# A hybrid layer on one core: differential attention weights carried to float32r tiles and transposed there, a mask on GpSimd, later transposes of the memory

## The chip, the cores and the metric

The kernel runs on one core of a Trainium2 chip. The metric is device time in microseconds (us) for one execution; the time given is the median of several runs. Five engines work in parallel, each in the order of its own instruction list: TensorE (PE), VectorE (DVE), ScalarE (ACT), GpSimd (POOL) and SyncE (SP), whose list issues nearly all transfers here. An engine that meets an instruction whose input or buffer isn't ready stands still, and everything behind it in that list stands with it.

## The reference

One layer, 1024 tokens of width 1024, float32. Three branches read the same normalised input and are merged by gates; the sum goes through an output matrix and a norm, and is added to the input. Cut to what the change touches:

```python
h = rms_norm(x, pre_w)                       # 1024 x 1024; then ten blocks of h @ w_in
# gated DeltaNet, 8 heads of 128, chunks: decay factors of a chunk, lower triangle only
gamma = jnp.exp(jnp.where(incl, G[..., :, None] - G[..., None, :], -jnp.inf))
# differential attention, 8 heads with two maps of width 64, 8 query blocks of 128
sc = jnp.einsum("bqhmd,bkhmd->bhmqk", q[:, start:end], k[:, :end]) * scale
p = jax.nn.softmax(sc + bias[None, :, None], axis=-1)
pd = (p[:, :, 0] - lam * p[:, :, 1])
outs.append(jnp.einsum("bhqk,bkhe->bqhe", pd, v[:, :end]))
# cross attention into a fixed memory of 256 rows
m = rms_norm(mem, mem_norm_w)
mk, mv = jnp.split(m @ w_mem_kv, 2, axis=-1)
# merge
y = gates[:, :, 0] * y_gdn + gates[:, :, 1] * y_diff + gates[:, :, 2] * y_mem
return x + rms_norm(y @ w_out, post_w)
```

## The kernel before, in words

The big products run in float32r. A weight block is loaded as float32, cast to a high part on ACT (line 167, `wh`) and its remainder is formed on DVE (line 169, `wl`); three matmuls for each piece (lines 219, 220, 224) then replace one of full precision.

The main program issues these products in order. Everything else is written as generators, threads that yield; a thread goes on by a step after a fixed number of the main program's matmuls, `pause(n)` waits for n steps, and a scheduler then settles the order of each engine's list when the program is built. So the order on each engine is fixed before the run, and a thread's instruction that comes too early for its input stops the engine.

The span has these stages. Up to about 545 us: the DeltaNet projections (`zmul` is the last kind of them), with threads for keys and queries (function `decay` loads decay rows, adds the mask `mneg`, and takes eight exponentials, line 468, in one go), for a triangular inverse, and for the scan over chunks (its end normalises two heads at a time on POOL, lines 691 and 692). From 545 to 680 us: `zmul(6)` and `zmul(7)`, beside them `mem_norm` (the memory's rows are normalised at line 760 and transposed at line 767) and `combine_tokens` (adds on POOL, lines 818 to 821, and on DVE), then the memory's values and keys (lines 795 to 797). From 680 to 1560 us: the other projections by a Strassen scheme (line 878, 3024 matmuls of 512 columns), and one thread that runs the 8 attention heads one after the other, then the memory's. From 1560 us: three branch products, the output product and the last norm.

In a head of the attention, query block i has w = 128 (i+1) keys. `scores(i)` makes both maps' scores in PSUM (lines 1142 and 1143) and adds the bias on DVE (line 1146); `exps(i)` takes both exponentials on ACT (line 1158); `combine(i)` forms p0 - lam p1 on DVE (line 1167); `turn(i)` transposes that on PE in blocks of 128 columns as plain float32 (line 1176), up to four blocks to a PSUM bank, and copies them back; `values(i)` multiplies them by v (line 1191). `turn` and `values` run one block behind `scores`. The head's v itself is transposed by `turned` (line 720), which uses float32r operands. A matmul operand of type float32r has to be written as such by its producer; a transfer can do that, since it copies bits.

Of the kernel before, what the change touches and what calls it, by code (L numbers as in the profile page):

```python
# [9 lines left out]
F32 = mybir.dt.float32  # L10
# [6 lines left out]
P = 128  # L17
# [28 lines left out]
def bm(ap, m):  # L46

    return ap.unsqueeze(1).to_broadcast([ap.shape[0], m, ap.shape[1]])
# [3 lines left out]
def hybrid_layer_kernel(  # L52
# [148 lines left out]
    def pause(n):  # L201
        for _ in range(n):
            yield
# [72 lines left out]
    with gx:  # L276
# [8 lines left out]
        tri = gp.tile([P, P], F32, name="tri")  # L285
        G.memset(tri, 1.0)
        G.affine_select(tri, tri, pattern=[[1, P]], compare_op=ALU.is_ge, fill=0.0, base=0, channel_multiplier=-1)
        mneg = gp.tile([P, P], F32, name="mneg")
        G.memset(mneg, 0.0)
        G.affine_select(mneg, mneg, pattern=[[1, P]], compare_op=ALU.is_ge, fill=NEG, base=0, channel_multiplier=-1)  # L290
        ones = gp.tile([P, P], F32, name="ones")
        G.memset(ones, 1.0)

# [167 lines left out]
        def decay(h, gm):  # L461

            nc.sync.dma_start(gm, gscr[0, 8 * h:8 * h + 8, :].rearrange("c i -> (c i)").partition_broadcast(P))
            yield from pause(2)
            V.tensor_tensor(gm, gm, bm(mneg, 8), op=ALU.add)
            yield from pause(1)
            for c in range(8):
                A.activation(gm[:, c], gm[:, c], AF.Exp, bias=negG[:, h, c:c + 1])
# [249 lines left out]
    def turned(out_, in_):  # L718

        T.transpose(out_.bitcast(F32R), in_, identr)  # L720

    def xtile(shape=(P, S), dt=F32):
        return xp.tile(list(shape), dt, name=nm("x"), tag="x", bufs=9)
# [20 lines left out]
    def mem_norm():  # L744

        mts = []
        for t in range(2):
            mt = rtile((P, D))
            nc.sync.dma_start(mt, mem[t * P:(t + 1) * P, :])
            mts.append(mt)  # L750
        for _ in range(2):
            mh.append(xtile((P, 4, MEM), F32R))
            ml.append(xtile((P, 4, MEM), F32R))
        sq = rtile()
        for mt in mts:
            ss = small([P, 1], "ss", 4)
            A.activation(sq, mt, AF.Square, accum_out=ss)
            rs = small([P, 1], "rs", 4)
            rpow(rs, ss, 1.0 / D, EPS, mhalf)
            V.tensor_scalar(mt, mt, rs, None, op0=MUL)  # L760
            yield
        yield from pause(3)
        for k2 in range(4):
            pt = sd()
            for kk in range(2):
                for t in range(2):
                    T.transpose(pt[:, 2 * kk + t], mts[t][:, (2 * k2 + kk) * P:(2 * k2 + kk + 1) * P], ident)
            for kk in range(2):
                k = 2 * k2 + kk
                src = pt[:, 2 * kk:2 * kk + 2].rearrange("p a b -> p (a b)")  # L770
                A.activation(mh[k // 4][:, k % 4], src, AF.Copy, scale=memw[:, k:k + 1])
                V.scalar_tensor_tensor(ml[k // 4][:, k % 4], src, memw[:, k:k + 1],
                                       mh[k // 4][:, k % 4].bitcast(F32), op0=MUL, op1=SUB)
            yield
        ready.add("mem")
# [317 lines left out]
    def diff_head(h):  # L1093
# [57 lines left out]
        def exps(i):  # L1151
            w = (i + 1) * P
            ng = small([P, 2], "ng", 4)
            V.tensor_scalar(ng, mxs.pop(i)[:, (w - 1) // 512], -scl, None, op0=MUL)  # L1154
            yield
            l1 = l1s[i] = small([P, 1], "l1", 4)
            for m, l in enumerate((l0[:, i:i + 1], l1)):
                A.activation(s[i][m][:, :w], s[i][m][:, :w], AF.Exp, bias=ng[:, m:m + 1], scale=scl, accum_out=l)  # L1158
                yield from pause(2)

        def combine(i):
            w = (i + 1) * P
            s0, s1 = s[i]
            c1 = small([P, 1], "c1", 4)
            V.reciprocal(c1, l1s.pop(i))
            V.scalar_tensor_tensor(c1, c1, l0[:, i:i + 1], nlam, op0=MUL, op1=MUL)
            V.scalar_tensor_tensor(s0[:, :w], s1[:, :w], c1, s0[:, :w], op0=MUL, op1=ADD)

        def turn(i):

            pT = s[i][1].rearrange("p (a b) -> p a b", b=P)
            for b in range(0, i + 1, 4):
                n = min(4, i + 1 - b)
                pp = sd()
                for c4 in range(n):
                    T.transpose(pp[:, c4], s[i][0][:, (b + c4) * P:(b + c4 + 1) * P], ident)  # L1176
                yield
                if b == 0:
                    A.copy(pT[:, b:b + n], pp[:, :n])
                else:  # L1180
                    V.tensor_copy(pT[:, b:b + n], pp[:, :n])
                yield

        def values(i):
            nonlocal o
            if i == 0:
                o = xtile((P, 8, P))
            pT = s.pop(i)[1].rearrange("p (a b) -> p a b", b=P)
            po = sd()
            for c in range(i + 1):  # L1190
                T.matmul(po[:, 0], lhsT=pT[:, c], rhs=vt[:, c], start=(c == 0), stop=(c == i))  # L1191
            yield from pause(2)
            A.copy(o[:, i], po[:, 0])
            A.activation(po[:, 0], po[:, 0], AF.Square, accum_out=sso[:, i:i + 1])
            yield

        for i in range(NT + 1):
            if i < NT:
                yield from scores(i)
            if i:  # L1200
                yield from turn(i - 1)
            if i < NT:
                yield from exps(i)
            if i:
                yield from values(i - 1)
            if i < NT:
                yield
                combine(i)
                yield from pause(3 if i < 2 else 1)
        spawn(diff_norm(h, o, l0, sso))  # L1210

    def diff_norm(h, o, l0, sso):
# [216 lines left out]
    for t in range(NT):  # L1429

        ts_ = slice(t * P, (t + 1) * P)
        po = pos[t] if t < 2 else columns()
        xr, res = xtile(), xtile()
        nc.sync.dma_start(xr, x[ts_, :])
        ss = small([P, 2], "oss", 4)
        for f, sl in enumerate(half):
            products(po, t, range(4 if t < 2 else 0, KT), f)
            A.activation(res[:, sl], po[f], AF.Square, scale=1.0 / 32, accum_out=ss[:, f:f + 1])
        rs = small([P, 1], "rs", 4)
        V.tensor_scalar(rs, ss[:, 0:1], ss[:, 1:2], EPS, op0=ADD, op1=ADD)  # L1440
        G.tensor_tensor(rs, rs, mhalf[:, 0:1], op=ALU.pow)
        for f, sl in enumerate(half):
            V.scalar_tensor_tensor(res[:, sl], po[f], rs, pw[:, sl], op0=MUL, op1=MUL)
            (V if f else G).tensor_tensor(res[:, sl], res[:, sl], xr[:, sl], op=ADD)
            nc.sync.dma_start(out[ts_, sl], res[:, sl])


# [22 lines left out]
```

## Time and profile before

| what | value |
|---|---|
| time, median of 3 runs | 1926.06 us (1922.33 to 1928.35) |
| profiled execution, its own time | 1924.15 us |
| span of that execution | 1922.4 us |
| PE busy | 1868.7 us, 97% of the span |
| DVE, ACT, POOL busy | 63%, 47%, 9% |
| mean granted TensorE clock | 0.99 |
| DMA, mean | 147 GB/s, 47.4% of 16 engines' time |

Busy time of PE is close to the span, so the time that PE stands still is the small difference, and it lies in few places. The other engines' busy shares say only that none of them is full on the mean; whether one of them is late at a given place is seen in the timeline there. The profiled execution's span and its own time differ by 1.75 us, which lie around the span.

### The profile page before, as it was taken

Reading aid. Unit: us, or ns where it says so; the run is one execution under the profiler, and the core shown is the slowest. Engines: PE = TensorE matmul, PEld = TensorE weight load, DVE = VectorE, ACT = ScalarE, POOL = GpSimd, SP = SyncE. Lnnn points to the kernel's source line nnn. Section 1 sums busy time; section 2 is a strip of 40 time slices with the busy share of each in tenths; the row PEclk is TensorE's granted clock in tenths of the full one; section 3 lists DMA queues with packets and bytes.
Section 4 is the critical chain, followed back from the end, with each engine's and each line's share of the span. In section 5 each row is a group of like instructions: output and inputs, shape, how many; then the busy total and the mean of one; then the engine's idle time right before and its main releaser. Section 6 shows DMA issues by size and latency. Waiting matters only on the chain.

```text
span 1922.4 us, 28495 instructions
## 1 busy us (share of the span) xinstructions
PE 1868.7 (97%) x10231; PEld 1561.9 (81%) x10231; DVE 1218.5 (63%) x2499; ACT 894.5 (47%) x1997; POOL 164.0 (9%) x131
## 2 busy tenths in 40 slices
PE   7999999999978999999999999999999999999998
PEld 5787888788866888888888888888888878888886
DVE  5688667855366676777777777766666662435432
ACT  5552664545444465555555565555444551212211
POOL 1130131302140100000000000000000000000011
PEclk9999999999989999999999999999999999999999
DMA  4232231322136675656657355443665586755422
GB/s 129 87 97 68 69 96 42 98 63 75 51 120 200 190 210 171 173 162 184 185 143 212 114 176 170 148 154 104 214 207 188 170 270 206 231 195 171 156 91 88
DMA packets 294018, 282.45 MB, mean 147 GB/s; under 512 B 41474, under 2 KB 226164, under 8 KB 293876
## 3 DMA queue, kind: packets, MB, share of 16 engines
q1 hardware_dynamic: 293876, 280.63, 47.4%
q8 instruction: 80, 1.31, 0.3%
q14 instruction: 62, 0.51, 0.1%
HBM read 189.27 MB, written 91.29 MB: 146 GB/s over the span
## 4 chain that ended last, share of the span: by engine, by line
PE 57%; issue 30%; DVE 8%; ACT 2%; DMA 2%; POOL 1%; SPq 0%; POOLq 0%; DVEq 0%; ACTq 0%
PE bank L878 27%; PE acc L224 4%; PE acc L220 4%; PE acc L219 4%; PE sd L1191 3%; PE sd L1143 2%; PE sd L1142 2%; PE sd L1176 2%; DVE o L437 1%; DVE wl L169 1%; PE sd L474 1%; DMA wr<-in_w_mem_kv_dram 1%; PE sd L661 1%; PE sd L673 1%; PE sd L668 1%
## 5 line engine op out<-in xcount | busy, mean ns | idle before, releaser
L878 PE MATMUL bank<-h,hi 128*128 128x512 f32 x864 | 283.7, 398 | 0.0
L167 ACT CAST wh<-wr 128x512 fp32r<-128x512 f32 x144 | 89.3, 620 | 281.6 <-PE acc L220 251.6
L219 PE MATMUL acc<-h,wh 128*128 128x512 f32 x468 | 194.1, 415 | 2.2 <-DVE rp L157 1.8
L220 PE MATMUL acc<-h,wh 128*128 128x512 f32 x468 | 186.7, 399 | 0.0
L878 PE MATMUL bank<-q,hi 128*128 128x512 f32 x576 | 186.4, 397 | 0.0
L878 PE MATMUL bank<-o,hi 128*128 128x512 f32 x576 | 185.2, 396 | 0.8 <-DVE u L965 0.4
L878 PEld LDWEIGHTS bank<-h,hi 128*128 128x128 f32 x864 | 159.5, 188 | 28.2
L878 PE MATMUL bank<-h,lo 128*128 128x512 f32 x432 | 171.4, 397 | 0.0
L224 PE MATMUL acc<-h,wl 128*128 128x512 f32 x468 | 159.4, 399 | 9.2 <-DVE wl L169 9.2
L169 DVE TENSOR_TENSOR wl<-wr,wh 128x512 fp32r<-128x512 f32 x144 | 102.7, 714 | 101.3 <-ACT wh L167 97.8
L864 ACT CAST hi<-wr 128x512 fp32r<-128x512 f32 x144 | 89.0, 618 | 133.2 <-PE bank L878 112.9
L868 DVE TENSOR_TENSOR lo<-wr,hi 128x512 fp32r<-128x512 f32 x144 | 98.9, 687 | 52.8 <-PE bank L878 39.8
L878 PEld LDWEIGHTS bank<-o,hi 128*128 128x128 f32 x576 | 106.4, 188 | 22.1 <-ACT u L883 1.2
L878 PEld LDWEIGHTS bank<-q,hi 128*128 128x128 f32 x576 | 107.0, 188 | 19.9
L878 PE MATMUL bank<-q,lo 128*128 128x512 f32 x288 | 114.5, 398 | 0.0
L878 PE MATMUL bank<-o,lo 128*128 128x512 f32 x288 | 114.2, 396 | 0.0
L224 PEld LDWEIGHTS acc<-h,wl 128*128 128x128 f32 x468 | 88.4, 191 | 29.1 <-DVE wl L169 11.3
L1158 ACT ACTIVATE x<-x,ng 128x256 f32<-128x256 f32 (+7 forms) x128 | 98.8, 774 | 24.7 <-DVE ng L1154 24.7
L864 ACT CAST hi<-raw 128x512 fp32r<-128x512 f32 x108 | 66.9, 619 | 84.9 <-PE bank L878 79.6
L219 PEld LDWEIGHTS acc<-h,wh 128*128 128x128 f32 x468 | 89.3, 191 | 17.4 <-issue 3.0
L220 PEld LDWEIGHTS acc<-h,wh 128*128 128x128 f32 x468 | 89.3, 191 | 14.5
L878 PEld LDWEIGHTS bank<-h,lo 128*128 128x128 f32 x432 | 81.4, 188 | 14.2
(361 smaller groups left out, 4125.3 us busy)
## 6 DMA issues: line engine op xcount, KB each, us to landing
raw<-in_w_in_dram SPq DMA_DIRECT2D x144, 256.0 KB, 3.8
wr<-in_w_in_dram SPq DMA_DIRECT2D x64, 256.0 KB, 2.8
qd<-u SPq DMA_DIRECT2D x128, 128.0 KB, 2.4
wl<-qd SPq DMA_DIRECT2D x64, 256.0 KB, 3.5
gts<-u SPq DMA_DIRECT2D x48, 256.0 KB, 3.2
u<-oscr SPq DMA_DIRECT2D x48, 256.0 KB, 4.6
raw<-gts SPq DMA_DIRECT2D x24, 512.0 KB, 4.4
o<-gscr SPq DMA_DIRECT2D x16, 512.0 KB, 4.9
```

What stands on the lines that cost most here:

```text
L167: A.copy(hi, raw)
L169: V.tensor_tensor(lo, raw, hi.bitcast(F32), op=ALU.subtract)
L219: T.matmul(ps[:, sl], lhsT=hi[:, kk], rhs=hh(k, f), start=(k == 0), stop=False)
L220: T.matmul(ps[:, sl], lhsT=hi[:, kk], rhs=hl(k, f), start=False, stop=False)
L224: T.matmul(ps[:, sl], lhsT=lo[:, kk], rhs=hh(k, f), start=False, stop=(k == 7))
L864: A.copy(self.hi[p], self.src[p])
L868: V.tensor_tensor(self.lo[p], self.src[p], self.hi[p].bitcast(F32), op=SUB)
L878: T.matmul(ps, lhsT=t[l][:, kk], rhs=comb[p][kk][r], start=(first and kk + n == 0), stop=(kk == 3 and n == 2), skip_group_check=True)
L1142: T.matmul(ps[m], lhsT=q4[:, m], rhs=ks[m][:, u:e], start=True, stop=False)
L1143: T.matmul(ps[m], lhsT=q4[:, 2 + m], rhs=ks[m][:, u:e], start=False, stop=True)
L1158: A.activation(s[i][m][:, :w], s[i][m][:, :w], AF.Exp, bias=ng[:, m:m + 1], scale=scl, accum_out=l)
L1191: T.matmul(po[:, 0], lhsT=pT[:, c], rhs=vt[:, c], start=(c == 0), stop=(c == i))
```

## The change

Five edits.

1. The mask of `decay`: the add of a tile of large negative numbers on DVE is replaced by a select on GpSimd (POOL) on the decay tile itself, 128x1024, 16 times; the mask tile `mneg` is no longer built.
2. `mem_norm` waits 9 steps in place of 3 before the transposes of the memory.
3. `combine(i)` is followed by a transfer `move(i)` on SP, which copies the weights' tile, 128 partitions by w float32, into a float32r tile of the same core's memory; 64 such transfers in all, 64 KB to 512 KB. `turn(i)` transposes the copy with `turned`, and the transposed blocks go to the tile that the weights were formed in. For w over 512 the second map's tile is given up before the copy's is taken.
4. In the loop over query blocks `exps(i)` stands right after `scores(i)`, `combine(i)` after `turn(i-1)`; the pause at a block's end is 2 steps for the first four blocks (before: 3 for two blocks, 1 for the others), and a step lies before each transfer.
5. In the last norm the product with the norm's weight is taken on DVE before the row's factor is known, the squares go back into PSUM, and one operation on DVE does the factor and the residual; before, a DVE operation and an add on POOL or DVE did.

```diff
-            V.tensor_tensor(gm, gm, bm(mneg, 8), op=ALU.add)
+            G.affine_select(gm, gm, pattern=[[0, 8], [1, P]], compare_op=ALU.is_ge, fill=NEG, base=0,
+                            channel_multiplier=-1)
...
-        yield from pause(3)
+        yield from pause(9)
         for k2 in range(4):
             pt = sd()
...
             V.scalar_tensor_tensor(s0[:, :w], s1[:, :w], c1, s0[:, :w], op0=MUL, op1=ADD)
+            del s0, s1
+            if w <= 512:
+                yield from move(i, s[i][0], xtile((P, 512), F32R))
+            else:
+                s[i][1] = None
+                yield from move(i, s[i][0], xtile(dt=F32R))
+
+        def move(i, src, dst):
+            w = (i + 1) * P
+            yield
+            s[i] = [src, dst]
+            nc.sync.dma_start(dst[:, :w].bitcast(F32), src[:, :w])
...
-                    T.transpose(pp[:, c4], s[i][0][:, (b + c4) * P:(b + c4 + 1) * P], ident)
+                    turned(pp[:, c4], s[i][1][:, (b + c4) * P:(b + c4 + 1) * P])
...
             if i < NT:
                 yield from scores(i)
+                yield from exps(i)
             if i:
                 yield from turn(i - 1)
             if i < NT:
-                yield from exps(i)
+                yield from combine(i)
             if i:
                 yield from values(i - 1)
-            if i < NT:
-                yield
-                combine(i)
-                yield from pause(3 if i < 2 else 1)
+            if i < 4:
+                yield from pause(2)
...
-            A.activation(res[:, sl], po[f], AF.Square, scale=1.0 / 32, accum_out=ss[:, f:f + 1])
+            V.tensor_tensor(res[:, sl], po[f], pw[:, sl], op=MUL)
+            A.activation(po[f], po[f], AF.Square, scale=1.0 / 32, accum_out=ss[:, f:f + 1])
...
-            V.scalar_tensor_tensor(res[:, sl], po[f], rs, pw[:, sl], op0=MUL, op1=MUL)
-            (V if f else G).tensor_tensor(res[:, sl], res[:, sl], xr[:, sl], op=ADD)
+            V.scalar_tensor_tensor(res[:, sl], res[:, sl], rs, xr[:, sl], op0=MUL, op1=ADD)
```

Lines of the changed kernel are named by its own numbers: the mask is line 462, the exponentials behind it 465, the scan's end 689 and 690, the memory's transposes 765, `turned` 718, the transfer 1177, the score products 1140 and 1141, the values 1201.

Three places of the engines' lists. First POOL, in the DeltaNet stage, where the scan's end of two heads (the two powers `sso` and the two scalings of `v`) stands. Before:

```order
L691 TENSOR_TENSOR sso_1862<-sso_1862,mhalf 128x8
L692 TENSOR_TENSOR v_1105<-v_1105,sso_1862 128x1024
L691 TENSOR_TENSOR sso_1863<-sso_1863,mhalf 128x8
L692 TENSOR_TENSOR v_1331<-v_1331,sso_1863 128x1024
L158 TENSOR_TENSOR nk<-rp_2607,phalf 128x8
L504 TENSOR_TENSOR o_2512<-o_2512,fj 128x1024
```

and now, where the three rows L462 are masks of decay tiles `o`:

```order
L689 TENSOR_TENSOR sso_1871<-sso_1871,mhalf 128x8
L690 TENSOR_TENSOR v_1110<-v_1110,sso_1871 128x1024
L689 TENSOR_TENSOR sso_1872<-sso_1872,mhalf 128x8
L690 TENSOR_TENSOR v_1338<-v_1338,sso_1872 128x1024
L462 AFFINE_SELECT o_2525<-o_2525 128x1024
L462 AFFINE_SELECT o_2648<-o_2648 128x1024
L462 AFFINE_SELECT o_2801<-o_2801 128x1024
```

The first mask of these, that of the tenth decay tile, now waits behind both powers and both scalings; before it was on DVE and waited for none of them.

Second PE, near the end of `zmul(6)`, where the memory's transposes (`raw` is a normalised memory tile) stood before; `acc_5237` is the accumulator of `zmul(6)`, `wl_5295` its second weight tile:

```order
L224 MATMUL acc_5237<-h_135,wl_5295 128x512 x2
L767 MATMUL sd_5317<-ident,raw_5250 128x128
L767 MATMUL sd_5332<-ident,raw_5250 128x128
L219 MATMUL acc_5237<-h_137,wh_5293 128x512
L220 MATMUL acc_5237<-h_138,wh_5293 128x512
L219 MATMUL acc_5237<-h_137,wh_5293 128x512
L220 MATMUL acc_5237<-h_138,wh_5293 128x512
L767 MATMUL sd_5317<-ident,raw_5252 128x128
L767 MATMUL sd_5317<-ident,raw_5250 128x128
```

Now they stand inside `zmul(7)` (`acc_5363`), behind the last product with its first weight tile `wl_5368`:

```order
L219 MATMUL acc_5363<-u_129,wh_5366 128x512
L220 MATMUL acc_5363<-u_130,wh_5366 128x512
L224 MATMUL acc_5363<-h_128,wl_5368 128x512
L224 MATMUL acc_5363<-u_129,wl_5368 128x512
L765 MATMUL sd_5402<-ident,raw_5277 128x128
L765 MATMUL sd_5402<-ident,raw_5279 128x128
L765 MATMUL sd_5402<-ident,raw_5277 128x128
L765 MATMUL sd_5402<-ident,raw_5279 128x128
L219 MATMUL acc_5363<-h_131,wh_5416 128x512
L220 MATMUL acc_5363<-h_132,wh_5416 128x512
L219 MATMUL acc_5363<-h_131,wh_5416 128x512
```

The transposes moved past the 6 matmuls that were left of `zmul(6)` and 24 of `zmul(7)`, and all four of a group now stand together.

Third SP, between the transfers of the first head's tiles 6 and 7 (both L1177); L1104 loads queries, L979 and L990 store the pieces of a later head's keys and queries, which have just left PSUM:

```order
L1177 DMA x_7158<-x_7068 128x896
L1104 DMA wl_7436<-qd_5221 128x512
L979 DMA kd_866_5208<-u_7204 64x512
L979 DMA kd_867_5209<-u_7204 64x512
L979 DMA kd_866_5208<-u_7205 64x512
L979 DMA kd_867_5209<-u_7205 64x512
L990 DMA qd_5222<-u_7239 64x4x128 x4
L990 DMA qd_5222<-u_7240 64x4x128 x4
L1177 DMA x_7276<-x_7178 128x1024
```

The second L1177 row stands behind one load and twelve stores; its transposes on PE wait for it. Before there was no transfer between a tile's weights and its transposes.

## Rows read from the trace of the kernel before

**Rows 1.** Windows: busy us of PE, PEld, DVE, ACT, POOL; granted clock, DMA share, GB/s.

```profile
545.00:680.00 135.00, 117.76 (x586) 95.81 (x586) 95.08 (x143) 64.41 (x117) 28.39 (x19) 0.95 0.60 181
...
680.00:1560.00 880.00, 876.39 (x4524) 735.77 (x4523) 619.02 (x1383) 477.38 (x1121) 13.14 (x8) 1.00 0.56 171
```

**Rows 2.** Timeline of PE, four stops: start, duration; idle before and releaser in brackets.

```profile
275.61 0.47 PE L219 MATMUL acc<-h,wh 128*128 128x512 f32 x1 [1.76 <-DVE rp L157]
...
365.41 1.22 PE L224 MATMUL acc<-h,wl 128*128 128x512 f32 x2 [4.46 <-DVE wl L169]
...
557.57 0.66 PE L767 MATMUL sd<-ident,raw 128*128 128x128 f32 x2 [8.97 <-issue]
...
579.42 0.80 PE L796 MATMUL acc<-wl,x 128*128 128x512 f32 x1 [2.89 <-DVE wl L169]
```

**Rows 3.** Groups of line 1176 and of line 720: duration ns min/median/max, first and last start.

```profile
L1176 PE MATMUL sd<-ident,x x288: 270/272/323, 681.3 to 1358.6; 128*128 128x128 f32 x144
...
L720 PE MATMUL sd<-identr,wh x64: 221/235/257, 677.1 to 1280.1; 128*128 128x128 f32 x64
```

**Rows 4.** Timeline of PE, four transposes of each kind and their neighbours.

```profile
677.05 0.45 PE L720 MATMUL sd<-identr,wh 128*128 128x128 f32 x4
677.34 0.69 PE L878 MATMUL bank<-o,hi 128*128 128x512 f32 x2
...
1000.95 0.40 PE L878 MATMUL bank<-q,lo 128*128 128x512 f32 x1
1001.18 0.60 PE L1176 MATMUL sd<-ident,x 128*128 128x128 f32 x4
1001.54 0.71 PE L878 MATMUL bank<-h,hi 128*128 128x512 f32 x2
```

**Rows 5.** Head 3, tile 7: last score product, weights formed (L1167), transposes (L1176).

```profile
1000.04 0.39 PE L1143 MATMUL sd<-x,wl 128*128 128x512 f32 x1
...
L1167 DVE SCALAR_TENSOR_TENSOR x<-x,c,x x1: 1285/1285/1285, 1007.7 to 1007.7; 128x1024 f32<-128x1024 f32 x1
...
L1176 PE MATMUL sd<-ident,x x8: 271/272/273, 1010.0 to 1011.7; 128*128 128x128 f32 x8
```

**Rows 6.** DMA issues of the page: operation, count, KB each, us to landing.

```profile
qd<-u SPq DMA_DIRECT2D x128, 128.0 KB, 2.4
...
raw<-gts SPq DMA_DIRECT2D x24, 512.0 KB, 4.4
```

**Rows 7.** Timeline of SP's queue: eight small stores in a row.

```profile
950.07 5.45 SPq L992 DMA_DIRECT2D qd<-u  x8
```

**Rows 8.** Groups of the mask add (line 465) and of a mask on GpSimd (L1075).

```profile
L465 DVE TENSOR_TENSOR o<-o,mneg x16: 1204/1224/2918, 62.6 to 442.3; 128x1024 f32<-128x1024 f32 x16
...
L1075 POOL TENSOR_SCALAR_AFFINE_SELECT x<-x x1: 1149/1149/1149, 634.8 to 634.8; 128x1024 f32<-128x1024 f32 x1
```

**Rows 9.** Timeline of POOL and ACT around two masks.

```profile
268.72 1.90 POOL L692 TENSOR_TENSOR v<-v,sso 128x1024 f32<-128x1024 f32 x1
...
350.94 4.08 POOL L692 TENSOR_TENSOR v<-v,sso 128x1024 f32<-128x1024 f32 x2
...
267.18 2.45 ACT L468 ACTIVATE o<-o,negG 128x128 f32<-128x128 f32 x8 [3.12 <-DVE o L465]
```

**Rows 10.** Timeline of DVE: one form of add at two speeds.

```profile
547.96 1.77 DVE L742 TENSOR_TENSOR o<-hi,o 128x512 fp32r<-128x512 f32 x1
549.65 0.68 DVE L742 TENSOR_TENSOR o<-lo,o 128x512 fp32r<-128x512 f32 x1
```

**Rows 11.** Timeline of DVE: a memory row normalised, a weight of the memory projection.

```profile
558.48 0.75 DVE L760 TENSOR_SCALAR raw<-raw,rs 128x1024 f32<-128x1024 f32 x1 [0.45 <-POOL rs L158]
...
578.69 0.68 DVE L169 TENSOR_TENSOR wl<-wr,wh 128x512 fp32r<-128x512 f32 x1
```

**Rows 12.** Timeline of DVE at the end of the span.

```profile
1916.61 1.41 DVE L1443 SCALAR_TENSOR_TENSOR x<-sd,rs,x 128x512 f32<-128x512 f32 x2 [0.66 <-POOL rs L1441]
...
1918.05 1.20 DVE L1444 TENSOR_TENSOR x<-x,x 128x512 f32<-128x512 f32 x1
```

More of the change, by code (lines that the diff above doesn't have):

```diff
@@ L287, in hybrid_layer_kernel @@
         G.affine_select(tri, tri, pattern=[[1, P]], compare_op=ALU.is_ge, fill=0.0, base=0, channel_multiplier=-1)
-        mneg = gp.tile([P, P], F32, name="mneg")
-        G.memset(mneg, 0.0)
-        G.affine_select(mneg, mneg, pattern=[[1, P]], compare_op=ALU.is_ge, fill=NEG, base=0, channel_multiplier=-1)
         ones = gp.tile([P, P], F32, name="ones")
@@ L1167, in combine @@
             V.scalar_tensor_tensor(s0[:, :w], s1[:, :w], c1, s0[:, :w], op0=MUL, op1=ADD)
+            del s0, s1
[9 more added lines that the diff above has]
+            nc.sync.dma_start(dst[:, :w].bitcast(F32), src[:, :w])
         def turn(i):
-            pT = s[i][1].rearrange("p (a b) -> p a b", b=P)
+            pT = s[i][0].rearrange("p (a b) -> p a b", b=P)
             for b in range(0, i + 1, 4):
@@ L1187, in values @@
                 o = xtile((P, 8, P))
-            pT = s.pop(i)[1].rearrange("p (a b) -> p a b", b=P)
+            pT = s.pop(i)[0].rearrange("p (a b) -> p a b", b=P)
             po = sd()
```

## Prediction

> **What bounds the kernel now.** The windows come first. From 680 to 1560 us, the Strassen stage with the attention beside it, PE is busy for 876.4 of 880 us at a granted clock of 1.00 [rows 1]: whatever is taken from PE's own work there shortens the span, and whatever makes PE wait there lengthens it. Between 545 and 680 us PE is busy for only 117.8 of 135 us, at a clock of 0.95 [rows 1]. Next I read the timeline of PE for its stops. Four of them matter: 8.97 us before the memory's transposes at 557.57, 2.89 us for a weight remainder from DVE at 579.42, 4.46 us for another one at 365.41, and 1.76 us at 275.61 [rows 2]. So the change has three fields: the cost of a transpose, what waits in the attention, and the stops outside it.
>
> **Transposes.** 288 float32 transposes (line 1176) become float32r ones, as the 64 of line 720 are now. Alone, a row lasts 272 against 235 ns in the median [rows 3], but neighbours overlap, so the distance to the next matmul counts. Four float32 ones hold it up from 1001.18 to 1001.54, 0.36 us; four float32r ones from 677.05 to 677.34, 0.29 us [rows 4]. That is 0.07 us for four, 18 ns each, and 288 x 18 ns = **-5.2 us**. The durations' difference of 37 ns would give -10.7; nothing at all is the other end. I take the distance, since both groups stand between the same kind of products.
>
> **The transfers.** Each tile's weights now go through SP and a transfer before PE may transpose them. I read head 3, tile 7. Its last score product starts at 1000.04, the weights are formed at 1007.7 + 1.285 = 1008.99, and the first transpose starts at 1010.0 [rows 5]. So the chain takes 8.95 us, PE has 9.96 us of other work ahead of the transpose, and the margin is 1.0 us. The changed list gives PE nearly the same work between the two: 32 products at 0.23 us (the step from 1000.95 to 1001.18 [rows 4]), seven transposes, seven products with v, together about 9.6 us. Counted in this way, the tile 7s of heads 0 to 7 have 13.9, 11.4, 13.9, 9.6, 10.5, 11.6, 9.6 and 10.2 us.
>
> No transfer of this kind is in the trace. The nearest rows are 2.4 us from issue to landing for 128 KB and 4.4 us for 512 KB [rows 6]; a last tile is 512 KB, tiles 1 to 6 lie between. With 2.4 us the chain needs 11.35 us, and PE stops for 1.75 + 0.85 + 1.75 + 1.15 = 5.5 us in heads 3, 4, 6 and 7. With 4.4 us it needs 13.35, and the sum over heads 1 and 3 to 7 is 1.95 + 3.75 + 2.85 + 1.75 + 3.75 + 3.15 = 17.2 us. Two things speak for the lower part: the two exponentials now stand ahead of the previous tile's copy on ACT, which shortens the chain, and head 3's is among the longest chains, so others need less. Tiles 0 to 6 have more time: their weights are smaller and their margin larger, and I give them nothing. I take **+7 us**.
>
> The queue is a second price. SP spends 5.45 us on eight stores, 0.68 us each [rows 7]. Behind one load and twelve stores, as tile 7 of head 0 stands, a transfer could issue up to 13 x 0.68 = 8.8 us late if the stores are released only then; in the lists some ten of 64 transfers stand behind eight or more. Most of these stores are released before the weights are formed, and head 0 has the largest supply, 13.9 us. In the sum this is nothing; in the upper end it is 5 us. The stores queued behind a waiting transfer feed tiles a head later, so their delay costs nothing as long as it stays under a head's time.
>
> **The mask.** The add took 1.22 us of DVE, 16 times [rows 8], 20 us in all; a select of the same size on GpSimd took 1.15 [rows 8]. The price lies in the list. The tenth mask now stands behind two powers and two scalings, the last of which ends at 268.72 + 1.90 = 270.6 [rows 9]. The select then ends at about 271.8 and its eight exponentials, 2.45 us, at about 274.2, where they ended at 267.18 + 2.45 = 269.6 before [rows 9]: 4.6 us late. Behind them on ACT are an operation of the convolution and a weight cast, and PE stops there already, until 275.61 [rows 2]. That stop grows by 2.5 to 4.6 us; I take 3.5. The 13th mask waits likewise until 350.94 + 4.08 = 355.0 [rows 9] and ends at 356.2. PE reaches the stop there only at 365.41 - 4.46 = 360.95 and waits for DVE, not ACT [rows 2], so I count nothing, at most 2. The freed DVE time can shorten this stop a little, and I take -0.5. Together **+3 us**, range 0 to 7.
>
> How much is DVE relieved? A two-input add of 128x512 took 0.68 us, and 1.77 while POOL was adding too [rows 10], 1.09 us more. A select on GpSimd beside such an add may thus cost back what the removed mask gave: 16 x 1.09 = 17 of 20 us. The Trainium skill, page "SBUF — State Buffer", section "Who interferes with whom", says so as a rule: a DVE instruction with two inputs in SBUF and a GpSimd instruction that reads SBUF share a port, and the later one waits for the whole of the other. By that rule the relief is 3 us of DVE time, without it 20. The two speeds in the trace agree with it.
>
> **The memory.** PE stops at 557.57 - 8.97 = 548.60 [rows 2]. In the new list 30 matmuls of 0.23 us come ahead of the transposes, so PE reaches them at about 555.5, later where the first of `zmul(7)`'s weights is late. The second normalised tile is there at 558.48 + 0.75 = 559.2 [rows 11]. So of 9 us some 3.7 stay, and 5.3 are won here. But after that PE already waits for DVE: the memory projection's weight is ready at 578.69 + 0.68 = 579.4 [rows 11], where PE stood still for 2.89 us [rows 2]. DVE works through the same list in between, and is busy for 95 us of this stage [rows 1]; a PE that comes 5 us earlier waits 5 us longer unless DVE is earlier too. I take **-1.5 us**, range 0 to -5.3.
>
> **The end.** The last two row operations and the add ran from 1916.61 to 1918.05 + 1.20 = 1919.25 [rows 12], 2.64 us; two operations of the first kind take 1.41 [rows 12]. That wins 1.2, and the squares now wait for the product ahead of them, about 0.7: **-0.5 us**, range 0 to -1.2. The mask tile that is no longer built costs nothing: its build lies beside the first loads.
>
> **Sum.** -5.2 + 7 + 3 - 1.5 - 0.5 = +2.8 us. On the profiled execution's own 1924.15 us (a span of 1922.4 and 1.75 around it) that is 1927; on the median of the runs, 1926.06, which is 0.1% higher, 1929. I forecast **1928 us**, no change that can be told.
>
> **Rivals.**
> - Faster: the transfers land behind other work after all. If the chain becomes shorter by as much as a short landing costs, the last tiles stop for 1 us in all, the memory's gain of 5.3 is kept because DVE has room, and the mask costs nothing: -5.2 + 1 - 5.3 - 0.5 = -10, 1916 us. For it speaks that margins other than the last tile's are larger; against it the 1.0 us in head 3 and the DVE list.
> - Slower: the landing decides. At 4.4 us each last tile is late as worked out: -5.2 + 17.2 + 3 - 1.5 - 0.5 = +13, 1940 us; with 5 more for the queue 1945. It ends beyond no change from a landing of about 3 us on, if the chain before it is as long as now. For it speaks the only 512 KB row; against it the two points above.
> - The change doesn't do what it says: float32r transposes of these tiles take as long as float32 ones. Then the 5.2 us are missing: +8, 1935 us. The 64 rows of line 720 speak against it.
>
> **How the numbers follow.** About 0.3%, 5.8 us, is what a measurement of this kernel can tell from no change. Chances: the forecast 0.38, faster 0.30, slower 0.24, no cheaper transposes 0.08. The forecast's own spread of some 6 us puts 0.03 of it on the faster side and 0.05 on the slower; of the faster rival 0.03 and of the slower one 0.03 stay within; of the last case half. That gives faster 0.30, same 0.37, slower 0.33 after rounding. The range runs from 1913, a little beyond the faster rival, to 1943, between the two ends of the slower one.
>
> **What would show it.** In the changed profile: four transposes of line 718 in the attention with 0.29 us to the next matmul, or 0.36; idle time of PE ahead of line 718 at tile 7 of heads 3, 4, 6 and 7 and none in heads 0 and 2; the landing time of the 512 KB copies; the stop at about 275 us grown to about 5; exponentials of the tenth mask ending at about 274; the 8.97 us stop gone, with a stop at the memory's weights of some 8 us in its place; 1.4 us in place of 2.6 at the end. The forecast is wrong if landings are far from 3 us, if DVE lets the memory's gain through, or if a late tile holds up the exponentials of the next and so the whole thread.

## The result and the profile after

The changed kernel takes 1937.45 us (median of 4 runs, 1935.62 to 1939.80), the kernel before 1927.19 in the same comparison. The ratio is 1.0056, with a 95% interval of 1.0041 to 1.0072: **10 us slower**, and clear of noise. The time lies inside the predicted range, 9 us over the forecast. It is near the figure of the slower rival, but late transfers, that rival's mechanism, are not what made it slow. One execution of the kernel before and one of c8 below took 2331 us, at a granted clock of 0.75; they are left out of every median and interval here.

The profiled execution took 1936.44 us with a span of 1934.4, 12.0 more than before. PE's first Strassen product starts at 625.3 us, where it was 614.4 before, and the last one at 1577.7, where it was 1564.7. So 10.9 of the 12 us are lost ahead of the first Strassen product.

First the windows, of the kernel before in two stretches that were not shown,

```profile
100.00:160.00 60.00, 59.00 (x299) 49.02 (x298) 54.67 (x106) 28.34 (x51) 18.81 (x15) 1.00 0.29 79
...
260.00:300.00 40.00, 37.55 (x215) 32.02 (x214) 24.40 (x59) 25.11 (x58) 15.89 (x8) 1.00 0.31 89
```

and of the changed kernel in the same two, then in its stage of the memory and its Strassen stage (columns as in [rows 1]):

```profile
100.00:160.00 60.00, 52.30 (x251) 42.82 (x250) 45.30 (x102) 31.62 (x51) 21.05 (x18) 0.94 0.26 71
...
260.00:300.00 40.00, 34.97 (x189) 29.51 (x188) 19.43 (x48) 24.23 (x54) 16.68 (x12) 0.96 0.29 83
...
555.00:692.00 137.00, 120.32 (x589) 96.21 (x588) 94.97 (x143) 63.87 (x117) 28.16 (x19) 0.94 0.59 180
...
692.00:1572.00 880.00, 872.58 (x4521) 729.81 (x4520) 617.56 (x1382) 474.82 (x1120) 13.47 (x8) 1.00 0.61 192
```

Between 100 and 160 us PE now works for 52.3 us in place of 59.0, at a clock of 0.94 in place of 1.00; between 260 and 300 us for 35.0 in place of 37.6. The stage of the memory gave 117.8 of 135 us before [rows 1] and gives 120.3 of 137 now. The Strassen stage is busy for 872.6 of 880 us.

The stops of PE in the changed kernel, in its timeline (as [rows 2]):

```profile
116.28 0.50 PE L219 MATMUL acc<-h,wh 128*128 128x512 f32 x1 [1.24 <-ACT wh L167]
...
121.84 0.79 PE L224 MATMUL acc<-h,wl 128*128 128x512 f32 x1 [4.36 <-DVE wl L169]
...
280.51 0.50 PE L219 MATMUL acc<-h,wh 128*128 128x512 f32 x1 [1.75 <-ACT wh L167]
...
284.98 0.77 PE L219 MATMUL acc<-h,wh 128*128 128x512 f32 x1 [3.28 <-DVE rp L157]
...
587.16 0.80 PE L793 MATMUL acc<-wh,x 128*128 128x512 f32 x1 [3.50 <-ACT wh L167]
591.34 0.79 PE L794 MATMUL acc<-wl,x 128*128 128x512 f32 x1 [3.39 <-DVE wl L169]
...
1100.47 0.89 PE L718 MATMUL sd<-identr,x 128*128 128x128 f32 x8 [1.55 <-DMA x<-x]
...
1269.77 0.54 PE L718 MATMUL sd<-identr,x 128*128 128x128 f32 x4 [1.67 <-DMA x<-x]
```

Before, there was no stop at 116 to 122 us. The one at 275 us (1.76 us, and 0.69 behind it for a weight remainder) has become 1.75 + 3.28. The 8.97 us stop ahead of the memory's transposes is gone; stops of 3.50 and 3.39 us at the memory's values stand in its place. In the attention, PE waits for a transfer (`DMA x<-x`), 1.55 and 1.67 us at two of the last tiles.

**The first loss** begins on ACT, 10 us ahead of the stop. The timeline of ACT before, with two masks' exponentials (eight each) between two weight casts:

```profile
104.02 0.62 ACT L167 CAST wh<-wr 128x512 fp32r<-128x512 f32 x1 [3.80 <-PE acc L220]
...
106.92 2.46 ACT L468 ACTIVATE o<-o,negG 128x128 f32<-128x128 f32 x8
...
110.24 2.44 ACT L468 ACTIVATE o<-o,negG 128x128 f32<-128x128 f32 x8
112.58 0.61 ACT L167 CAST wh<-wr 128x512 fp32r<-128x512 f32 x1
```

and after:

```profile
105.17 0.40 ACT L466 ACTIVATE o<-o,negG 128x128 f32<-128x128 f32 x1 [2.98 <-POOL o L462]
105.59 1.28 ACT L436 ACT_TABLE_LOAD   x1
106.88 1.06 ACT L436 ACTIVATE o<-o 128x1024 f32<-128x1024 f32 x1
107.96 1.28 ACT L466 ACT_TABLE_LOAD   x1
109.26 2.16 ACT L466 ACTIVATE o<-o,negG 128x128 f32<-128x128 f32 x7
...
112.28 2.44 ACT L466 ACTIVATE o<-o,negG 128x128 f32<-128x128 f32 x8
114.62 1.10 ACT L432 ACTIVATE v<-acc,cols 128x1024 f32<-128x1024 f32 x1
115.62 1.13 ACT L167 CAST wh<-wr 128x512 fp32r<-128x512 f32 x2
```

The fourth mask's exponentials (line 466 by the trace, not 465) start earlier, since the select is done sooner, but only one of the eight stands there: then comes an activation of the convolution (line 436), with a table load ahead of it and another behind, then the other seven. The weight cast that stood first, at 104.02, now stands last, at 115.62, behind both masks and another convolution activation, and PE stops for 1.24 us for it. Its remainder, which DVE formed at 108.16 before, follows only at 121.14. The cast is done at about 116.2; DVE's list has three operations of the convolution (line 434) and small ones ahead of the remainder, and DVE works through them without a pause. The longer stop, 4.36 us until 121.84, waits for that:

```profile
119.84 1.27 DVE L434 SCALAR_TENSOR_TENSOR v<-acc,cols,v 128x1021 f32<-128x1021 f32 x1
...
121.14 0.64 DVE L169 TENSOR_TENSOR wl<-wr,wh 128x512 fp32r<-128x512 f32 x1
```

No engine is full here: DVE is busy for 45.3 of these 60 us, ACT for 31.6. With the select on GpSimd the scheduler has written the lists of ACT and DVE in another order, and the cast and the remainder that PE needs next have come behind work that PE does not need.

The stops have a second price. Behind them PE's granted clock is at its lower level, 0.50 or 1.2 GHz, until about 127.5 us. Six matmuls run in two microseconds there, ten once it is 1.00 again:

```profile
124.00:126.00 2.00, 2.00 (x6) 1.52 (x6) 0.47 (x1) 0.00 (x0) 2.00 (x4) 0.50 0.31 53
...
128.00:130.00 2.00, 2.00 (x10) 1.66 (x9) 0.49 (x1) 0.62 (x1) 0.46 (x1) 1.00 0.85 246
```

The twelve products from 122.43 to 127.50 take 5.1 us; at 0.23 us each they would take 2.8, so by this estimate the clock costs some 2 us more.

**The second loss** is the one that the prediction worked out. The timelines of POOL and of ACT at the tenth mask:

```profile
273.52 1.90 POOL L690 TENSOR_TENSOR v<-v,sso 128x1024 f32<-128x1024 f32 x1
275.38 3.19 POOL L462 TENSOR_SCALAR_AFFINE_SELECT o<-o 128x1024 f32<-128x1024 f32 x3
```

```profile
276.50 2.45 ACT L466 ACTIVATE o<-o,negG 128x128 f32<-128x128 f32 x8 [6.67 <-POOL o L462]
...
279.86 1.13 ACT L167 CAST wh<-wr 128x512 fp32r<-128x512 f32 x2
```

The select waits behind the scan's last scaling until 275.4, ACT stands still for 6.67 us for it, and the exponentials, the convolution and two casts follow. Before, the exponentials ended at 269.6 [rows 9], here at 278.95, 9.3 us later. The scan's scaling itself ends 4.8 us later than before (275.4 against 270.6), since the whole stage is late by then; the other 4.5 us are the wait behind it, for which the prediction had worked out 4.6.

**The attention.** From the list of DMA issues, the transfers of 512 KB (us to landing last), and in PE's timeline head 3's tile 7, from its last score product to the first four new transposes and the matmul behind them; then the weights formed (L1165) and all the new transposes (L718):

```profile
x<-x SPq DMA_DIRECT2D x8, 512.0 KB, 4.1
```

```profile
1003.71 0.39 PE L1141 MATMUL sd<-x,wl 128*128 128x512 f32 x1
...
1013.49 0.46 PE L718 MATMUL sd<-identr,x 128*128 128x128 f32 x4
1013.78 0.46 PE L876 MATMUL bank<-q,hi 128*128 128x512 f32 x1
```

```profile
L1165 DVE SCALAR_TENSOR_TENSOR x<-x,c,x x1: 1283/1283/1283, 1008.7 to 1008.7; 128x1024 f32<-128x1024 f32 x1
```

```profile
L718 PE MATMUL sd<-identr,x x288: 218/233/327, 695.4 to 1356.7; 128*128 128x128 f32 x144
```

The 512 KB copies land in 4.1 us, near the upper end that was assumed. But the chain ahead of them has become shorter: in head 3, tile 7, from the score product at 1003.71 to the weights at 1008.7 + 1.28 = 1010.0 it takes 6.3 us, where it took 8.95 before [rows 5]. In ACT's timeline the two exponentials start 2.2 us after the score product in place of 3.0, and the weights are formed 0.5 us behind the second one in place of 2.4, so most of this comes from the new place of `combine`. PE stopped for 1.55 and 1.67 us in heads 4 and 6 and not at all in head 3; with 0.76 and 0.29 us at two other tiles these are all its stops for a transfer, 4.3 us. A transpose lasts 233 ns in place of 272 [rows 3], and four hold PE up from 1013.49 to 1013.78, 0.29 us, as worked out.

The end, in DVE's timeline:

```profile
1927.37 0.69 DVE L1447 TENSOR_TENSOR x<-sd,x 128x512 f32<-128x512 f32 x1 [4.75 <-PE sd L1428]
...
1929.81 1.41 DVE L1453 SCALAR_TENSOR_TENSOR x<-x,rs,x 128x512 f32<-128x512 f32 x2 [0.72 <-POOL rs L1451]
```

The product with the weight is taken at 1927.37, ahead of the factor, and the last two operations take 1.41 us where they took 2.64 [rows 12].

### The profile page after: what moved, and what is told of

Read it like the earlier page. It is cut to its first block, busy times and chain, and to the rows that moved or that the text cites. A ratio compares the mean times of both kernels' runs of the same rounds, so it can differ in the third digit from the quotient of the medians.

```text
span 1934.4 us, 28743 instructions
## 1 busy us (share of the span) xinstructions
PE 1869.7 (97%) x10231; PEld 1560.3 (81%) x10231; DVE 1197.4 (62%) x2491; ACT 900.3 (47%) x2003; POOL 166.5 (9%) x137
## 4 chain that ended last, share of the span: by engine, by line
PE 84%; DVE 6%; DMA 4%; issue 3%; ACT 2%; POOL 1%; SPq 0%; DVEq 0%; POOLq 0%; ACTq 0%
PE bank L876 33%; PE acc L224 9%; PE acc L219 9%; PE acc L220 9%; PE sd L1428 5%; PE sd L1201 3%; PE sd L1141 2%; PE sd L1140 2%; PE sd L718 1%; PE sd L1302 1%; PE sd L1269 1%; DMA x<-x 1%; PE sd L472 1%; DVE wl L169 1%; DMA u<-oscr 1%
## 5 line engine op out<-in xcount | busy, mean ns | idle before, releaser
L876 PE MATMUL bank<-h,hi 128*128 128x512 f32 x864 | 279.5, 397 | 0.0
L224 PE MATMUL acc<-h,wl 128*128 128x512 f32 x468 | 159.7, 400 | 12.5 <-DVE wl L169 12.5
```

What stands on the lines that cost most here:

```text
L224: T.matmul(ps[:, sl], lhsT=lo[:, kk], rhs=hh(k, f), start=False, stop=(k == 7))
L876: T.matmul(ps, lhsT=t[l][:, kk], rhs=comb[p][kk][r], start=(first and kk + n == 0), stop=(kk == 3 and n == 2), skip_group_check=True)
```

## The experiments

Each kernel is compared with runs of the kernel before on the same chip.

| kernel | us, median | before | ratio, 95% interval |
|---|---|---|---|
| c1, mask back on DVE | 1926.16 | 1926.34 | 1.0002, 0.9990 to 1.0013 |
| c2, mask edit alone | 1939.73 | 1926.34 | 1.0065, 1.0050 to 1.0080 |
| c3, 4th and 5th mask alone | 1933.09 | 1926.34 | 1.0029, 1.0017 to 1.0042 |
| c4, the other 14 masks | 1936.30 | 1926.34 | 1.0048, 1.0033 to 1.0063 |
| c5, ten masks | 1932.10 | 1926.03 | 1.0028, 1.0014 to 1.0043 |
| c6, attention alone | 1923.97 | 1926.03 | 0.9986, 0.9976 to 0.9996 |
| c7, no transfer, weights in float32r | 1921.88 | 1926.03 | 0.9976, 0.9963 to 0.9989 |
| c8, order of the attention alone | 1925.54 | 1926.03 | 0.9995, 0.9985 to 1.0005 |
| c9, select and a DVE pass | 1936.29 | 1928.08 | 1.0042, 1.0025 to 1.0059 |
| c10, without mask edit and pause | 1925.09 | 1928.08 | 0.9989, 0.9979 to 1.0000 |
| c11, memory's pause alone | 1929.68 | 1928.08 | 1.0013, 1.0002 to 1.0024 |
| c12, c7 and the end | 1922.09 | 1927.53 | 0.9975, 0.9965 to 0.9984 |

**Which edit.** c1 is the changed kernel with

```diff
-            G.affine_select(gm, gm, pattern=[[0, 8], [1, P]], compare_op=ALU.is_ge, fill=NEG, base=0, ...)
+            V.tensor_tensor(gm, gm, bm(mneg, 8), op=ALU.add)
```

> The changed kernel with its mask back on DVE; the other four edits stay. Theory A (the mask edit is the loss, since it re-sorts the engines' lists in the DeltaNet stage): about 10 us below the changed kernel, 1927 us, and no drift against the kernel before at 545 us. Theory B (the transfers are the loss): it stays within 3 us of the changed kernel, 1934 to 1940 us.

c2 is the kernel before with that edit the other way round, and no mask tile:

```diff
-            V.tensor_tensor(gm, gm, bm(mneg, 8), op=ALU.add)
+            G.affine_select(gm, gm, pattern=[[0, 8], [1, P]], compare_op=ALU.is_ge, fill=NEG, base=0, ...)
```

> The kernel before with the mask edit alone. Theory A: all of the loss is here, 8 to 11 us over the kernel before, 1935 to 1938 us. Theory B: at most the 3 us of the prediction, up to 1930 us.

c1 comes back to the time of the kernel before; c2 loses 13.4 us alone, more than theory A's 8 to 11. The mask edit is the whole loss, and the four other edits together give nothing that can be told. Theory B has fallen.

**Which masks.** c3 and c4 split the sixteen calls:

```diff
+            calls.append(h)
+            if len(calls) not in (4, 5):      # c3; c4 has: in (4, 5); c5: in (4, 5, 10, 11, 12, 13)
                 V.tensor_tensor(gm, gm, bm(mneg, 8), op=ALU.add)
+            else:
+                G.affine_select(gm, gm, pattern=[[0, 8], [1, P]], ...)
```

> The kernel before with only the 4th and 5th of the 16 masks on GpSimd. In the list of ACT a weight cast then stands behind both masks' exponentials and a convolution operation, with added table loads. Theory A1 (this one place of ACT's list is the price): a stop of 4 us or more on PE near 117 us and 6 to 11 us over the kernel before. Theory A2 (masks that wait in GpSimd's own list behind the scan's end, the 10th and the 13th, are the price): no loss, within 2 us of the kernel before.

> The kernel before with 14 masks on GpSimd, all but the 4th and 5th. ACT's list near 110 us is then that of the kernel before. Theory A1: within 3 us of the kernel before, no stop near 117 us. Theory A2: 3 to 10 us over it, with the stop near 278 us grown by some 3 us as in the changed kernel. If the select's port is the price (each select holds up DVE), the loss is spread: about 14 sixteenths of the full loss, 9 us.

PE's stops, first in c3, then in c4:

```profile
121.82 0.80 PE L224 MATMUL acc<-h,wl 128*128 128x512 f32 x1 [4.34 <-DVE wl L169]
...
281.58 0.47 PE L219 MATMUL acc<-h,wh 128*128 128x512 f32 x1 [1.82 <-DVE rp L157]
...
283.44 0.74 PE L224 MATMUL acc<-h,wl 128*128 128x512 f32 x2 [0.69 <-DVE wl L169]
```

```profile
278.36 0.50 PE L219 MATMUL acc<-h,wh 128*128 128x512 f32 x1 [1.76 <-ACT wh L167]
...
282.82 0.76 PE L219 MATMUL acc<-h,wh 128*128 128x512 f32 x1 [3.27 <-DVE rp L157]
```

Each place has its own masks. With the 4th and 5th alone on GpSimd the stop of 4.34 us near 122 is there (1.24 ahead of it), the one at 281 us is as before (1.82 + 0.69), and 6.8 us are lost. With the other fourteen there is no stop near 122, the one at 278 us has grown to 1.76 + 3.27, and 10.0 us are lost, of which the 2.6 us by which that stop has grown are only a part. So both A1 and A2 hold a part; A1's expectation for c4, within 3 us, was wrong, and so was A2's for c3, no loss. The two losses add up to 16.8 us, more than the 13.4 of all masks together; why they lose less together is not shown.

> The kernel before with ten masks on GpSimd: the 4th, 5th and the 10th to 13th stay on DVE, so none stands behind the scan's end of GpSimd's list and ACT's list near 110 us is as before. If the two places (the cast behind the exponentials, the masks behind the scan's end) make up the whole loss: within 3 us of the kernel before, 1924 to 1929 us, the stop near 278 us back to 2 to 3 us in all. If every select costs (port, or the same wait in small), 10 sixteenths of 13 us: 8 us over, 1934 us.

c5 keeps the masks of both places on DVE and still loses 6.1 us, so the expectation that the two places make up the whole loss was wrong. PE's two stops, each with a row of DVE ahead of it:

```profile
148.69 0.68 DVE L169 TENSOR_TENSOR wl<-wr,wh 128x512 fp32r<-128x512 f32 x1
149.42 0.73 PE L224 MATMUL acc<-h,wl 128*128 128x512 f32 x2 [2.19 <-DVE wl L169]
...
363.99 1.15 DVE L536 TENSOR_TENSOR q<-q,y 128x192 f32<-128x192 f32 x1
...
372.69 1.22 PE L224 MATMUL acc<-h,wl 128*128 128x512 f32 x2 [5.61 <-DVE wl L169]
```

The stop near 280 us is 2.08 + 0.47, as without the edit. Two others have grown: one of 2.19 us near 149, where the kernel with the mask on DVE (c1) stops for 0.57, and one of 5.61 where [rows 2] has 4.46. The first waits for a remainder that DVE takes at 148.69, behind operations of the convolution and others, although its cast was done at 139.5. (Another weight cast has moved in ACT's list, from 144.96 to 149.87, but it starts when this stop is over.) Ahead of the second, two DVE operations on 128x192 take 1.46 and 1.15 us, beside an add and a select of GpSimd; before they took 0.36 and 1.34. That is 0.9 of the 1.15 us by which this stop has grown. The two stops explain some 2 of the 6 us. In this profile PE also ran at a granted clock of 0.50 from 214 to 220 us, without a stop of PE ahead of it and in no other profile, by estimate 3 us. The rest of c5 stays open.

c4 and c5 differ in the masks 10 to 13 alone, by 3.9 us. So the first place costs 6.8 us alone, the second 3.9, and the other ten masks 6.1, for which no one place is found.

**List or queue.** c9 keeps all 16 selects on GpSimd and adds behind each

```diff
+            V.tensor_scalar(gm, gm, 0.0, None, op0=ALU.add)
```

> The kernel before with all 16 selects on GpSimd, and behind each a pass of DVE over the same tile that adds 0, so that the exponentials again wait for DVE. By the lists, ACT's order near 110 us, its casts and table loads are then those of the kernel before, while the 10th mask still stands behind the scan's end on GpSimd. Theory L (the price is the place of weight casts in ACT's list): within 4 us of the kernel before, no stop near 117 us. Theory Q (the price is the wait in GpSimd's list, or the port): 10 us or more over it, as in c2, with the stop near 278 us at 5 us or more.

```profile
278.08 0.79 PE L219 MATMUL acc<-h,wh 128*128 128x512 f32 x1 [3.33 <-ACT wh L167]
...
282.50 0.77 PE L219 MATMUL acc<-h,wh 128*128 128x512 f32 x1 [2.34 <-DVE rp L157]
...
370.16 0.50 PE L219 MATMUL acc<-h,wh 128*128 128x512 f32 x1 [1.82 <-ACT wh L167]
...
374.90 1.22 PE L224 MATMUL acc<-h,wl 128*128 128x512 f32 x2 [3.54 <-DVE wl L169]
```

The exponentials wait for DVE again, ACT's list near 110 us is that of the kernel before, and the stop near 122 is gone, as theory L says, although masks 4 and 5 are selected on GpSimd. The stop at 278 us is 3.33 + 2.34, and another at 370 us is 1.82 + 3.54 (4.46 before [rows 2]), as theory Q says. In total 8.2 us are lost, between the 4 of theory L and the 10 of theory Q. So the first loss is the order of the lists and the second the queue behind the scan's end. I had set the two against each other; both are there. Not all of the 8.2 us is the mask's: for its added passes DVE waits for GpSimd three times between 61 and 68 us, 5.0 us in all, and the stop near 76 us grows from 3.49 to 5.47.

**The attention.** c6 is the kernel before with edits 3 and 4 alone, as the diff of the change has them:

```diff
+                yield from move(i, s[i][0], xtile(dt=F32R))
...
+                    turned(pp[:, c4], s[i][1][:, (b + c4) * P:(b + c4 + 1) * P])
...
+                yield from exps(i)          # right behind scores(i)
```

> The kernel before with the attention's edits alone (transfers, float32r transposes, the order of exponentials). By the changed kernel's trace (transposes -5.2 us, four stops of PE ahead of a tile's transposes, 5 us in all): 0 us, from -2 to +2, 1924 to 1928 us. By the prediction's sum +1.8 us.

c7 forms the weights straight into the float32r tile,

```diff
-            V.scalar_tensor_tensor(s0[:, :w], s1[:, :w], c1, s0[:, :w], op0=MUL, op1=ADD)
-            ... (the transfer)
+            dst = xtile((P, 512), F32R) if w <= 512 else xtile(dt=F32R)
+            V.scalar_tensor_tensor(dst[:, :w], s1[:, :w], c1, s0[:, :w], op0=MUL, op1=ADD)
+            s[i] = [s0, dst]
```

> As c6, but with no transfer: the weights are formed straight into a float32r tile on DVE, which rounds them there, and transposed from it. This leaves out the copy's exactness, so its time is that of cheaper transposes with no transfer at all. If the transfers cost the 5 us of their stops: 5 us below c6, 1921 us. If they are free: the same as c6.

and c8 keeps plain float32 transposes with the new order.

```diff
-                yield from move(i, s[i][0], xtile(dt=F32R))
-                    turned(pp[:, c4], s[i][1][:, (b + c4) * P:(b + c4 + 1) * P])
+                    T.transpose(pp[:, c4], s[i][0][:, (b + c4) * P:(b + c4 + 1) * P], ident)
```

> As c6, but with float32 transposes from the tile itself and no transfer: only the exponentials' place, the step and the pauses are changed. If the transposes win 5.2 us and the order nothing: the time of the kernel before, 5 us over c7. If the order itself wins or loses, c8 differs from the kernel before by that much.

c7 is 3.7 us under c8: that is what the transposes win. c6 is 2.1 us over c7, and in c6's profile PE's stops for a transfer add up to 2.0 us; but the intervals of c6 and c7 overlap, so that the runs alone exclude neither 0 nor 5 us. The order alone is within noise. The length of the stage decides nothing here: from the first to the last Strassen product it takes 950.5 us in c8, 951.3 in c6 and 947.9 in c7, but with the attention as before 950.2 in the kernel before and 954.5 in c4.

**The memory.** c11 is the kernel before with the longer pause alone.

```diff
-        yield from pause(3)
+        yield from pause(9)
         for k2 in range(4):
```

> The kernel before with 9 steps ahead of the memory's transposes alone. By the changed trace (the 9 us stop gone, 4.3 us won there, the same lost at the memory projection's weights): 0 to +2.5 us. By the prediction: -1.5 us.

```profile
555.39 0.50 PE L224 MATMUL acc<-h,wl 128*128 128x512 f32 x1 [1.82 <-DVE wl L169]
...
562.08 0.55 PE L767 MATMUL sd<-ident,raw 128*128 128x128 f32 x3 [1.52 <-DVE raw L760]
...
579.55 0.79 PE L795 MATMUL acc<-wh,x 128*128 128x512 f32 x1 [4.29 <-ACT wh L167]
583.72 0.79 PE L796 MATMUL acc<-wl,x 128*128 128x512 f32 x1 [3.38 <-DVE wl L169]
```

The 8.97 us stop has become 1.82 + 1.52 (and 1.41 behind them, for another remainder), and the memory's values, for which PE stopped for 2.89 us before [rows 2], now stop it for 4.29 + 3.38. Their weights come when ACT and DVE get to them, not earlier; DVE is busy for 33.5 of the 37 us from 555 to 592. The edit loses 1.6 us by the medians.

**Better than both.** c10 takes the mask edit and the pause out of the changed kernel.

```diff
-            G.affine_select(gm, gm, pattern=[[0, 8], [1, P]], ...)
+            V.tensor_tensor(gm, gm, bm(mneg, 8), op=ALU.add)
...
-        yield from pause(9)
+        yield from pause(3)
```

> The changed kernel with the mask on DVE and 3 steps ahead of the memory's transposes again: the attention's edits and the end's stay. From c6 (-2.7 us) and 0.4 us at the end: 3 us under the kernel before, 1923 us. If the memory's pause won anything in c1, this is slower than c1; if it cost something, faster by as much, up to 3 us.

c12 is c7 with the new end.

```diff
+            V.tensor_tensor(res[:, sl], po[f], pw[:, sl], op=MUL)
+            A.activation(po[f], po[f], AF.Square, scale=1.0 / 32, accum_out=ss[:, f:f + 1])
...
+            V.scalar_tensor_tensor(res[:, sl], res[:, sl], rs, xr[:, sl], op0=MUL, op1=ADD)
```

> The kernel before with the weights formed straight into a float32r tile (rounded there, no transfer, float32r transposes, the changed order of exponentials) and the end's edit; mask and memory as before. From c7, 4.6 us under the kernel before, and 0.4 us at the end: 5 us under it, 0.997. If c7's gain was chance, 1 to 3 us under it, as c8 and c10.

c10 is 3.0 us under the kernel before, at the edge of what its interval shows. c12 is 5.4 us under it and 15 us under the changed kernel; its weights are formed as float32r, which neither kernel does, so it is not the same computation.

## Why the prediction was right or wrong

The range held the time, but the likeliest case, no change, did not come: the sum was 2.8 us, the measured difference 10.3. By its terms:

- **The mask, +3 us: the step that failed.** It measured +13.4 us (c2), and with its range, 0 to 7, it was too low. The queue behind the scan's end was right: 2.5 to 4.6 us were worked out for the stop at 275, and it grew by 2.6, from 2.45 to 5.03. But the step looked only at GpSimd's list, where the mask had gone, and not at the lists of the engines that wait for it. "I count nothing" for the 13th mask held in the changed kernel, whose stop there is 4.06 us, at another matmul, in place of 4.46; in c9 it grew by 0.9. The place near 110 us, where on ACT a weight cast changed places with sixteen exponentials and two table loads came in, and on DVE its remainder fell behind the convolution, could be read from the lists before the run; the prediction did not read it. It cost 6.8 us alone (c3), the masks 10 to 13 some 3.9; for the 6.1 of the other ten masks the cause stays open for the most part.
- **The relief of DVE, -0.5 us within it**, can't be told apart. DVE's busy time fell from 1218.5 to 1197.4 us, and by the mask alone to 1201.8 (c2): 16.7 of the 20 us were freed, not the 3 of a select that holds up an add each time, and nothing came of it. In the changed kernel's trace the DVE instructions beside the 16 selects take at most 4.1 us longer in all than the shortest of their form, and beside 13 of the selects less than 0.3 each. So the shared port is no price of every select; it shows at single places, as near 364 us in c5. A price for each select would also give 1.7 us for two masks, where c3 lost 6.8.
- **The transposes, -5.2 us:** 3.7 by c7 against c8. The distance between neighbours was the right measure; the durations' difference would have given -10.7.
- **The transfers, +7 us:** 2.1 by c6 against c7, not clear of noise; PE's stops for a transfer are 2.0 us in c6's profile and 4.3 in the changed kernel's. The landing was near the upper end, 4.1 us, which by the prediction's sums means about 15 us. (4.4 us was not the only 512 KB row, as the prediction says: the kernel before has others, from 2.9 to 6.5 us.) The chain was the mis-sized part: it took 6.3 us in place of 8.95. That it would be shorter was named as a reason, by the exponentials' new place, and given no size; most of it came from the earlier `combine`. That the slower rival hangs on the landing alone was wrong for the same reason.
- **The memory, -1.5 us:** +1.6 by c11. The mechanism was right (4 to 5 us won at the transposes, given back at the memory's weights), but the term kept a third of the gain, and nothing was left.
- **The end, -0.5 us:** 1.2 us at the last operations, less the product ahead of the squares. The last PE product is 12.4 us late and the span 12.0 longer, so some 0.4 us were won in this profile; in those of c1, c10 and c12, which have the same end, the span ends as long after the last product as before, within 0.05 us. So it is 0.4 us at most.

With what was measured alone for each, 13.4 - 2.1 + 1.6 - 0.4 = 12.5 us, against 10.3 for all of them together. The chances were also added up wrongly: by the parts that the prediction lists, no change has 0.40 and slower 0.30, not 0.37 and 0.33.

## What to carry to other kernels

Where a scheduler writes the engines' lists, moving an operation to an idle engine changes the lists of all engines that wait for it; compare those lists for the few rows that the bottleneck needs next (here the weight casts and their remainders), and count the table loads. An idle engine with an in-order list is free only where nothing long stands ahead of the moved operation. When a stop goes, follow the work to the next place where the same engine waits: if that is fed by an engine that was busy nearly all the while, as DVE was here, little or nothing is won.

## What was not expected of the hardware

The same stop was followed by a different granted clock in different executions. In the kernel before, the stop at 275 us was followed by a clock of 1.00 between 260 and 300 us (first windows above). In c11, with the same list there, the stops were as long, and the window reads

```profile
260.00:300.00 40.00, 37.49 (x195) 31.55 (x194) 22.00 (x49) 24.61 (x56) 14.92 (x8) 0.91 0.31 87
```

0.91. Against the kernel before, the same product of PE comes 3.0 us later at 300 us than at 270. Of the other kernels with the mask on DVE, c1, c6, c7, c8 and c10 have 0.91 to 0.96 in this window and only c12 has 1.00, so the profile that the prediction was read from was not the usual one here. Profiles of one list differ by up to 3 us at this place, and a stage's time from two profiles is worth no more than that; the medians of many runs decide.
